# A weight ring of ten 2 MB pairs in place of nine, with areas taken from head tiles, the scatter matrix and overflow scratch

## The chip, the cores and the metric

The kernel runs on one core of a Trainium2 chip. The metric is the device time of one execution in microseconds. The profile was taken on one execution of the same program.

## The reference

All arrays are float32, with 256 tokens of width 1024. Two blocks follow each other:

```
x = x + mix(rmsnorm(x)) @ w_out            # pooling mixer beside latent attention
h = rmsnorm(x)
top4 = top_k(h @ w_router + b_router, 4)   # 32 experts, softmax over the four
x = x + sum_e gate_e * (swiglu(h @ w_gate_up[e] + b_gate_up[e]) @ w_down[e] + b_down[e])
x = rmsnorm(x)
# block 2: modulation from c @ w_ada, three kinds of attention, then a gated FFN of width 2816
```

An expert has 2048 columns of gate and up weights over 1024 rows (8 MB) and a down matrix of 1024 by 1024 (4 MB). All 32 experts are read: 384 MB of the 494 MB that the kernel moves.

## The kernel before, in words

**Stages.** `head()` computes the first mixer and the routing, `moe()` the 32 experts one after the other, `block2()` the second block. Each stage has its own pool of tiles in SBUF (`hp`, then `mp` with `ep`, then `bp`); they lie on the left side, above the constants and the ring, one in the place of the other. `ep` lies on the right side and ends at the end of the space. A tile of a later pool waits for the last readers and writers of those earlier tiles that lie on its addresses (`reuse_waits="tile"`), and for no others.

**The ring.** Weights go through slots of 1 MB (8,192 bytes per partition). Slots are numbered so that 2i and 2i+1 are the two halves of area `space[i]`; slot 12 is a single one, `space[6]` having half the size. A list, `loads`, holds all loads in the order in which the program needs them. `pump()` (line 227) gives the next load the first free slot, or the first free pair if it is larger than 1 MB, and issues its DMA on SyncE, whose program order is kept; it stops when there is none. `release()` frees slots and calls `pump()`. So every load waits, on SyncE, for the last reader of its slots, and behind it wait all later loads.

**Depth.** In the head the slots are 0 to 9 and 12; the areas 10 and 11 hold activations. `deepen()` (line 263) is called at the start of `moe()`: it adds three areas `extra0` to `extra2` in `ep` (slots 14 to 19) and slots 10 and 11, and then nine pairs are in use. An expert takes four loads of 2 MB for gate and up (`gu`, e, k) and two for down (`dn`, e, k); they are loaded as gu(e), dn(e-1). From gu(31,4) on (`LAST`), only slots 0 to 5 and 8 are given out (`KEPT`), since the others change their use in block 2.

**Addresses.** Bytes per partition, as the allocator places them in the kernel before:

| what | from | to |
|---|---|---|
| slot 12 | 104,416 | 112,608 |
| start of the left pools (`scr` in `hp`, `Pm` in `mp`) | 145,376 | |
| `hT` | 147,584 | 151,680 |
| `wh`, three buffers of 4,096 | 152,032 | 164,320 |
| `wl`, three buffers of 4,096 | 164,320 | 176,608 |
| router weights `wrt` | 176,768 | 177,792 |
| `extra0`, `extra1`, `extra2` | 180,192 | 229,344 |

The routing (line 939) takes the second and third `wl` buffer again for `eq`, one for each half of the tokens, writes their first 512 bytes and reduces them at line 957.

**The order of an expert.** In `gate_up(e)` 64 matmuls of 64 weight columns accumulate; a pair is released after each second k. At k = 1 the products of expert e-2 are scattered back, at k = 5 the activations of e-1 are transposed. `down(e-1)` follows. For each group of four experts `select` (line 1006) compares ranks with a counter into `Pm`; GpSimd copies `Pm` twice side by side into the tile `gF`, and `scat_T` (line 1059) transposes that into the scatter matrix `ST`. The bias of the down projection is loaded as one small load after gu(1,6) and added at expert 1.

**Overflow.** After expert 20 the kernel tests on all engines whether an expert has more than 64 tokens, and if so computes the rest in `overflow()` (line 1227). The inputs don't reach that.

Of the kernel before, what the change touches and what calls it, by code (L numbers as in the profile page):

```python
# [10 lines left out]
F32 = mybir.dt.float32  # L11
F32R = mybir.dt.float32r
BF = mybir.dt.bfloat16
# [7 lines left out]
P = 128  # L21
T = 256
NT = 2
# [15 lines left out]
SPL = (6, 7, 12)  # L39
BIG = (10, 11)  # L40
YAT = 9
EXTRA = (14, 15, 16, 17, 18, 19)

VECS = (("g_attn_norm", 8), ("g_q_a", 2), ("g_kv_a", 1), ("g_out_pool", 4), ("g_out_attn", 4), ("g_ffn_norm", 8),
        ("norm1_g_2", 8), ("norm2_g_2", 8), ("ml_conv_w_2", 16), ("ml_conv_b_2", 4), ("c_2", 8), ("ml_h_g_2", 2),
# [103 lines left out]
ADA = [(0, 2048, k, 1) for k in range(8)] + [(2048, 2048, k, 1) for k in range(8)] + [  # L149
    (4096, 1024, k, 2) for k in range(0, 8, 2)] + [(5120, 1024, k, 2) for k in range(0, 8, 2)]  # L150
HEAD = ('ada', 'ada', 'ada', 'pool', 'ada', 'ada', 'ada', 'ada', 'ada', 0, 1, 4, 6)
BD_AT = (1, 6)
MODE = "ddddpppp" "pppppppp" "ddpp" "pppp"
GRPS = (0, 8, 16, 20, 24)
STEPS = (3, 2, 0, 0)
# [12 lines left out]
class Net:  # L168
    def __init__(self, ctx, tc, a, out):
        self.tc, self.nc, self.a, self.out = tc, tc.nc, a, out  # L170
        self.const = ctx.enter_context(tc.tile_pool(name="const", bufs=1))
        self.ringp = ctx.enter_context(tc.tile_pool(name="ring", bufs=1))
        self.uid = 0
        self.space = [None] * 7
        self.phase(F32, 0, 1, 2, 3, 4, 6)
        self.phase(F32R, 5)
        self.slots, self.held_by = sorted(KEPT + SPL + (YAT,)), {}
        self.kept = set(KEPT)
        self.turn = {"s": 0, "b": 0, "c": 0}

        self.ps = ctx.enter_context(tc.tile_pool(name="ps", bufs=4, space=PSUM))
        self.loads, self.tiles = [], {}
        self.issued = 0
# [60 lines left out]

    def phase(self, dt, *which):
        for i in which:
            self.space[i] = self.ringp.tile([P, RING_W * (1 if i == 6 else 2)], dt, name=self.nm("ring"), tag=f"ring{i}", bufs=1)

    def next_of(self, tag, dt=F32R):
        i = self.turn[tag]  # L250
# [11 lines left out]

    def deepen(self, ep):
        self.phase(F32, 5)
        self.space += [ep.tile([P, 2 * RING_W], F32, name=f"extra{i}") for i in range(len(EXTRA) // 2)]
        self.slots += EXTRA + BIG
        self.pump()

    def chunk(self, key):
        return self.tiles[key]  # L270
# [275 lines left out]
    def head(self):  # L546
        nc, c = self.nc, self.const
        tl = self.tl
        with self.tc.tile_pool(name="hp", bufs=1, reuse_waits="tile") as hp:
            scr = tl(hp, [P, D], "scr", 1, BF)  # L550
            self.route_tiles(hp)
            Hh = self.big([P, KD, T], F32R)
# [444 lines left out]
    def moe(self):  # L997
        nc, c, tl = self.nc, self.const, self.tl
        with self.tc.tile_pool(name="mp", bufs=1, reuse_waits="tile") as mp, \
                self.tc.tile_pool(name="ep", bufs=1, side="right", reuse_waits="tile") as ep:  # L1000
            self.deepen(ep)
            xg, ST, pend = {}, {}, {}
            PM, PD = {}, {}
            acts, turned = {}, {}

            def select(g):
                e0 = g * GRP
                Pm = tl(mp, [P, NT, GRP, CAP], "Pm", 1, F32R)
                for tt in range(NT):
                    nc.vector.tensor_tensor(Pm[:, tt], self.rk[:, tt, e0:e0 + GRP][:, :, None].to_broadcast([P, GRP, CAP]),  # L1010
                                            self.iota_c[:, None, :].to_broadcast([P, GRP, CAP]), op=OP.is_equal)
                PM[g] = Pm
                PD[g] = tl(mp, [P, NT, GRP, 2, CAP], "gF", 1)
                for tt in range(NT):
                    for s in range(2):
                        nc.gpsimd.tensor_copy(PD[g][:, tt, :, s], Pm[:, tt])

            def scale(g):
                rg = tl(mp, [P, 512], "rg")[:, :GRP * CAP]
                p = self.tr()  # L1020
                for tt in range(NT):
                    self.mm(p[:, :256], self.rf[:, tt:tt + 1].to_broadcast([P, P]),
                            PM[g][:, tt].rearrange("p a b -> p (a b)").bitcast(F32), tt == 0, tt == 1)
                nc.scalar.copy(rg, p[:, :256])
                return rg
# [32 lines left out]

            def scat_T(g):
                s_ = tl(mp, [P, GRP, T], "ST", 1, F32R)  # L1060
                Pd = PD.pop(g)
                for e in range(0, GRP, 2):
                    p = self.tr()
                    for j in range(2):
                        for tt in range(NT):
                            nc.tensor.transpose(p[:, j * T + tt * P:j * T + (tt + 1) * P],
                                                Pd[:, tt, e + j].rearrange("p a b -> p (a b)"), self.ident)
                    nc.vector.tensor_copy(s_[:, e:e + 2, :], p.rearrange("p (a b) -> p a b", a=2))
                ST[g] = s_

# [32 lines left out]
            def down(e):  # L1103
                aT = turned.pop(e)
                pd = self.tr()
                n = 2 if e == E - 1 else 4
                for k in range(KD):
                    w = self.chunk(("dn", e, k - k % n))
                    for s in range(2):
                        nc.tensor.matmul(pd[64 * s:64 * s + 64, :], lhsT=aT[:, k % 4, (k // 4) * 64:(k // 4) * 64 + 64],  # L1110
                                         rhs=w[:, k % n, s * 512:(s + 1) * 512], start=k == 0, stop=k == KD - 1,
                                         skip_group_check=True)
                    if k % n == n - 1:
                        self.release(("dn", e, k + 1 - n))
                yh, yl = tl(mp, [P, 512], "ys", 1, F32R), tl(mp, [P, 512], "yl", 1, F32R)
                i = nc.scalar.copy(yh, pd)  # L1116
                j = nc.vector.tensor_tensor(yl, pd, yh, op=OP.subtract)  # L1117
                if e == E - 1:
                    keep = self.tc.keep_in_program_order
                    keep(i)  # L1120
                    keep(j)
                    self.phase(F32R, 3, 5, 6)
                    w = self.chunk(("fv", 0))
                    self.pre = [(w[:, 2 * q:2 * q + 2, :], *self.halves(w[:, 2 * q:2 * q + 2, :], self.pair("bs"[q])))
                                for q in range(2)]
                    for w, hi, lo in self.pre:
                        keep(nc.scalar.copy(hi, w))
                pend[e] = yh, yl
# [34 lines left out]
            for e in range(E):  # L1163
                hooks = {}
                if e - 2 in pend:
                    hooks[SCAT_AT] = lambda e=e: scatter(e - 2)
                if e - 1 in acts:
                    hooks[TURN_AT] = lambda e=e: turn(e - 1)
                gate_up(e, rg, hooks)
                rg = None  # L1170
                if e - 1 in turned:
                    down(e - 1)
                if e == 0:
                    self.counts(mp)
                    self.late_constants()
                if e % GRP == 1 and e // GRP not in ST:
                    scat_T(e // GRP)
                if e == 1:
                    b_down()
                if e % GRP == GRP - 2 and e // GRP + 1 < E // GRP:  # L1180
                    select(e // GRP + 1)
                    rg = scale(e // GRP + 1)
                if e in (OVF, E - 1):
                    turn(e)
                    scatter(e - 1)
                    if e // GRP not in ST:
                        scat_T(e // GRP)
                    down(e)
                if e == OVF:
                    scatter(e)  # L1190
                    self.overflow(mp)
                if e == E - 3:
                    self.gF = tl(mp, [P, D], "gF")
                    self.rowbc(self.gF, self.vcol("g_final", 0, KD))
            self.y = self.granule(YAT).rearrange("p (a b) -> p a b", a=NT)
            self.s = self.const.tile([P, NT, 4], F32, name="sz")
            scr = tl(mp, [P, D], "gc", 1, BF)

            def sums(tt, h):
                x, y, s = self.x, self.y, self.s[:, tt]  # L1200
# [23 lines left out]
        nc.vector.scalar_tensor_tensor(sg, sg, 1.0, uc, op0=OP.add, op1=OP.mult)  # L1224
        return sg

    def overflow(self, mp):
        nc, tc, a = self.nc, self.tc, self.a
        wm = a["moe"]
        bg = a["b_gate_up"].rearrange("l e n -> (l e) n")  # L1230
# [6 lines left out]
        def expert(e, tt, hT):  # L1237
            pd = [self.acc(), self.acc()]
            for n in range(2):
# [7 lines left out]
                gu = []  # L1247
                for i in range(2):
                    c = i * 1024 + n * 512
                    b = mp.tile([P, 512], F32, name=self.nm("ob"), tag=("rg", "ys")[i], bufs=1)  # L1250
                    nc.sync.dma_start(b, bg[bass.ds(e, 1), c:c + 512].to_broadcast([P, 512]))
                    nc.vector.tensor_tensor(b, ps[i], b, op=OP.add)
                    gu.append(b)
# [15 lines left out]
        m = nc.values_load(self.cmax[0:1, 0:1], min_val=0, max_val=T)  # L1269
        with tc.If(m > CAP):  # L1270
            for tt in range(NT):
                hT = self.tl(mp, [P, KD, P], "gF", 1)
                for g in range(0, KD, 4):
                    h = self.tl(mp, [P, 512], "ys", 1)
                    sl = slice(g * P, g * P + 512)
                    nc.vector.tensor_tensor(h, self.hh[:, tt, sl], self.hl[:, tt, sl], op=OP.add)
                    nc.vector.tensor_scalar(h, h, self.rf[:, tt:tt + 1], None, op0=OP.mult)
# [54 lines left out]
    def block2(self):  # L1332
        nc, x, tl = self.nc, self.x, self.tl
        with self.tc.tile_pool(name="bp", bufs=1, reuse_waits="tile") as bp:
            s, y = self.s, self.y
            v = tl(bp, [P, NT, 2], "vz")
            self.adat = iter(ADAT + (20,) * 20)
# [506 lines left out]
def build(ctx, tc, a, out):  # L1844
# [1 line left out]
    n.plan_loads()  # L1846
    n.last = [l[0] for l in n.loads].index(LAST)
    n.constants()
    n.pump()
    n.ada_setup()  # L1850
    n.head()
    n.moe()
    n.block2()
# [23 lines left out]
```

## Time and profile before

| | us |
|---|---|
| runs | 1409.63, 1412.65, 1408.57 (median 1409.63) |
| the profiled execution | 1412.59 |
| its span, first to last instruction | 1410.9 |

| engine | busy us | share of the span |
|---|---|---|
| TensorE (PE) | 1301.2 | 92% |
| VectorE (DVE) | 556.1 | 39% |
| ScalarE (ACT) | 313.1 | 22% |
| GpSimd (POOL) | 61.4 | 4% |

The DMA engines moved 494.00 MB, 349 GB/s over the span. The head ends at about 115 us, the experts at about 1045 us. A busy PE is not a PE at its peak, since matmuls are pipelined. DMA share is the mean busy share of the 16 DMA engines and can come out a little above 1.

### The profile page before, as it was taken

The page shows a single profiled execution, that of the slowest core. Times are in us where ns is not written, and L with a number is a line of the kernel's source. Part 1 is how long each engine was busy: PE and PEld are TensorE (multiplying, and loading weights), DVE is VectorE, ACT ScalarE, POOL GpSimd, SP SyncE. Part 2 cuts the span into 40 slices and gives each one's busy share as a digit, 9 for nine tenths or more (in the row PEclk, how much of TensorE's full clock was granted, in tenths as well). Part 3 has the DMA queues.
Part 4 walks back from the last instruction along what each step waited for, and adds up shares of the span by engine and source line. Part 5 has one row for each costly group of instructions (what it writes and reads, how often), then busy time and mean ns, then how long its engine had stood idle before and what let it go on. Part 6 is the DMA issues. An engine that isn't in the chain of part 4 may idle for free. (4 is left out here: it accounts for less than half of the span.)

```text
span 1410.9 us, 16725 instructions
## 1 busy us (share of the span) xinstructions
PE 1301.2 (92%) x6758; PEld 699.4 (50%) x6759; DVE 556.1 (39%) x1164; ACT 313.1 (22%) x603; POOL 61.4 (4%) x194
## 2 busy tenths in 40 slices
PE   7898999999999989889878998988889999999998
PEld 6675343333333333224222433323238887799997
DVE  6664323323222223122211322222247877655555
ACT  5561000000000000000000000000035556544443
POOL 5401000000000000000000000000000000000000
PEclk9999999999999999999999999999999999999999
DMA  9679999999999999999998999999997464545520
GB/s 346 236 288 381 428 428 425 428 425 428 425 428 426 427 427 426 427 426 428 425 425 362 427 426 427 426 427 428 421 369 311 175 249 154 209 176 192 193 98 30
DMA packets 43811, 494.00 MB, mean 350 GB/s; under 512 B 6192, under 2 KB 6320, under 8 KB 10064
## 3 DMA queue, kind: packets, MB, share of 16 engines
q1 hardware_dynamic: 41808, 492.12, 84.1%
q8 instruction: 55, 0.90, 0.3%
q10 hardware_dynamic: 1920, 0.75, 0.2%
q14 instruction: 28, 0.23, 0.0%
HBM read 491.81 MB, written 1.05 MB: 349 GB/s over the span
## 5 line engine op out<-in xcount | busy, mean ns | idle before, releaser
L1082 PE MATMUL acc<-ring,xg 128*64 128x512 f32 x1408 | 326.0, 608 | 22.9 <-DMA ring<-in_moe_dram 21.9
L1082 PEld LDWEIGHTS acc<-ring,xg 128*64 128x64 f32 x1408 | 98.0, 139 | 225.8 <-issue 181.9
L1110 PE MATMUL tr<-ring,aT 128*64 128x512 f32 x688 | 154.7, 596 | 7.4 <-DMA ring<-in_moe_dram 6.7
L301 DVE TENSOR_TENSOR ring<-ring,ring 128x1024 fp32r<-128x1024 f32 (+4 forms) x108 | 121.1, 1130 | 87.4 <-ACT ring L300 84.0
L1082 PE MATMUL acc<-extra,xg 128*64 128x512 f32 x640 | 147.4, 609 | 6.2 <-DMA extra<-in_moe_dram 6.2
L286 PEld LDWEIGHTS tr<-cols,ring 128*128 128x128 f32 x1056 | 128.1, 192 | 1.7 <-ACT cols L1327 0.8
L286 PE MATMUL tr<-cols,ring 128*128 128x256 f32 x1056 | 128.9, 283 | 0.0
L300 ACT CAST ring<-ring 128x1024 fp32r<-128x1024 f32 (+4 forms) x108 | 104.1, 974 | 103.9 <-PE tr L286 65.9
L1141 DVE SCALAR_TENSOR_TENSOR x<-tr,G,x 128x512 f32<-128x512 f32 x128 | 87.7, 744 | 76.5 <-PE tr L1137 76.5
L1220 DVE TENSOR_SCALAR gc<-acc 128x512 f32<-128x512 f32 x32 | 22.1, 691 | 239.6 <-PE acc L1082 239.6
L1117 DVE TENSOR_TENSOR yl<-tr,ys 128x512 fp32r<-128x512 f32 x32 | 22.1, 691 | 205.7 <-ACT ys L1116 205.7
L1110 PEld LDWEIGHTS tr<-ring,aT 128*64 128x64 f32 x688 | 48.3, 137 | 98.5 <-issue 85.1
L1221 ACT ACTIVATE sg<-gc 128x512 f32<-128x512 f32 x32 | 20.2, 631 | 339.6 <-DVE gc L1220 339.6
L1082 PEld LDWEIGHTS acc<-extra,xg 128*64 128x64 f32 x640 | 44.6, 140 | 96.6 <-issue 82.2
L1110 PE MATMUL tr<-extra,aT 128*64 128x512 f32 x336 | 76.1, 597 | 2.2 <-DMA extra<-in_moe_dram 1.9
L1116 ACT CAST ys<-tr 128x512 fp32r<-128x512 f32 x32 | 18.7, 585 | 240.6 <-PE tr L1110 240.6
L1099 ACT ACTIVATE aT<-tr 128x512 f32<-128x512 f32 x32 | 19.1, 597 | 232.6 <-PE tr L1097 232.6
L286 PE MATMUL acc<-ring,cols 128*128 128x384 f32 (+3 forms) x384 | 69.3, 330 | 1.2 <-ACT cols L1327 0.6
L286 PEld LDWEIGHTS acc<-ring,cols 128*128 128x128 f32 x384 | 61.3, 188 | 9.0 <-issue 5.7
L1037 DVE SCALAR_TENSOR_TENSOR xg<-tr,vt,rg 128x256 f32<-128x256 f32 x60 | 26.2, 479 | 91.3 <-PE acc L1082 74.6
L286 PE MATMUL acc<-ring,q 128*128 128x512 f32 x176 | 56.7, 394 | 0.0
L286 PE MATMUL acc<-wh,ring 128*128 128x512 f32 (+1 forms) x128 | 42.3, 410 | 4.0 <-ACT wh L307 3.8
(432 smaller groups left out, 1294.7 us busy)
## 6 DMA issues: line engine op xcount, KB each, us to landing
ring<-in_moe_dram SPq DMA_DIRECT2D x129, 2048.0 KB, 34.4
extra<-in_moe_dram SPq DMA_DIRECT2D x61, 2048.0 KB, 35.0
ring<-in_rest_dram SPq DMA_DIRECT2D x69, 1024.0 KB, 6.9
ring<-in_rest_dram SPq DMA_DIRECT2D x11, 768.0 KB, 5.7
ring<-in_moe_dram SPq DMA_DIRECT2D x4, 1024.0 KB, 12.8
ring<-in_rest_dram SPq DMA_DIRECT2D x2, 832.0 KB, 9.7
ring<-in_rest_dram SPq DMA_DIRECT2D x2, 780.0 KB, 12.1
ring<-in_rest_dram SPq DMA_DIRECT2D x3, 512.0 KB, 8.5
```

The source lines that it names most:

```text
L286: self.nc.tensor.matmul(out, lhsT=l, rhs=r, start=start, stop=stop, skip_group_check=True)
L300: i = nc.scalar.copy(hi, w)
L301: j = nc.vector.tensor_tensor(lo, w, hi, op=OP.subtract)
L1037: nc.vector.scalar_tensor_tensor(x[:, j, :], p[:, j * 256:(j + 1) * 256], self.vcol("g_ffn_norm", k + j), rg, op0=OP.mult, op1=OP.mult)
L1082: nc.tensor.matmul(d[64 * s:64 * s + 64, :], lhsT=xg[g, k - k % 2][:, k % 2, i * CAP:(i + 1) * CAP], rhs=w[:, o + s * 512:o + (s + 1) * 51 ...
L1099: nc.scalar.activation(aT.rearrange("p a b -> p (a b)"), p, AF.Copy, scale=0.5)
L1110: nc.tensor.matmul(pd[64 * s:64 * s + 64, :], lhsT=aT[:, k % 4, (k // 4) * 64:(k // 4) * 64 + 64], rhs=w[:, k % n, s * 512:(s + 1) * 512], ...
L1116: i = nc.scalar.copy(yh, pd)
L1117: j = nc.vector.tensor_tensor(yl, pd, yh, op=OP.subtract)
L1141: ins = nc.vector.scalar_tensor_tensor(d, p, self.G[:, tt, e:e + 1], d, op0=OP.mult, op1=OP.add)
L1220: nc.vector.tensor_scalar(gc, pg, 7.0, None, op0=OP.min)
L1221: nc.scalar.activation(sg, gc, AF.Tanh, scale=0.851)
```

## The change

`EXTRA` gets slots 20 and 21, a fourth area of `ep`, and ten pairs serve the experts. Slot 12 leaves the ring's own pool and is a tile of the stage's pool: the first of `hp` in the head, and of `bp` in block 2; during the experts it doesn't exist. The copy of `Pm` in `gF` falls away: `scat_T` multiplies `Pm` by the identity, once for each half of the output partitions. The tiles `ys` and `yl` fall away: the two halves of the down projection's result use `gc` and `uc` of the SwiGLU. The row of the final norm's gains takes the place of `hh`. The overflow branch takes as its scratch the pair of dn(20,4), which is released after the test, not before. The bias of the down projection is loaded after gu(9,6) and added at expert 9. The first `pump()` and `ada_setup()` are called at the start of `head()`.

```diff
-EXTRA = (14, 15, 16, 17, 18, 19)
+EXTRA = (14, 15, 16, 17, 18, 19, 20, 21)
...
-BD_AT = (1, 6)
+BD_AT = (9, 6)
...
-        self.phase(F32, 0, 1, 2, 3, 4, 6)
+        self.phase(F32, 0, 1, 2, 3, 4)
...
-            self.space[i] = self.ringp.tile([P, RING_W * (1 if i == 6 else 2)], dt, name=self.nm("ring"), tag=f"ring{i}", bufs=1)
+            self.space[i] = self.ringp.tile([P, RING_W * 2], dt, name=self.nm("ring"), tag=f"ring{i}", bufs=1)
...
     def deepen(self, ep):
         self.phase(F32, 5)
+        self.slots.remove(12)
         self.space += [ep.tile([P, 2 * RING_W], F32, name=f"extra{i}") for i in range(len(EXTRA) // 2)]
         self.slots += EXTRA + BIG
         self.pump()
+
+    def borrow(self, pool, dt):
+        self.space[6] = pool.tile([P, RING_W], dt, name=self.nm("ring"))
...
         with self.tc.tile_pool(name="hp", bufs=1, reuse_waits="tile") as hp:
+            self.borrow(hp, F32)
+            self.pump()
+            self.ada_setup()
             scr = tl(hp, [P, D], "scr", 1, BF)
...
                 PM[g] = Pm
-                PD[g] = tl(mp, [P, NT, GRP, 2, CAP], "gF", 1)
-                for tt in range(NT):
-                    for s in range(2):
-                        nc.gpsimd.tensor_copy(PD[g][:, tt, :, s], Pm[:, tt])
 
             def scale(g):
-                rg = tl(mp, [P, 512], "rg")[:, :GRP * CAP]
+                rg = tl(mp, [P, GRP * CAP], "rg")
...
             def scat_T(g):
                 s_ = tl(mp, [P, GRP, T], "ST", 1, F32R)
-                Pd = PD.pop(g)
                 for e in range(0, GRP, 2):
                     p = self.tr()
                     for j in range(2):
                         for tt in range(NT):
-                            nc.tensor.transpose(p[:, j * T + tt * P:j * T + (tt + 1) * P],
-                                                Pd[:, tt, e + j].rearrange("p a b -> p (a b)"), self.ident)
+                            for s in range(2):
+                                self.mm(p[64 * s:64 * s + 64, j * T + tt * P:j * T + (tt + 1) * P],
+                                        PM[g][:, tt, e + j].bitcast(F32), self.ident, True, True)
                     nc.vector.tensor_copy(s_[:, e:e + 2, :], p.rearrange("p (a b) -> p a b", a=2))
                 ST[g] = s_
...
-                    if k % n == n - 1:
+                    if k % n == n - 1 and (e, k) != (OVF, KD - 1):
                         self.release(("dn", e, k + 1 - n))
-                yh, yl = tl(mp, [P, 512], "ys", 1, F32R), tl(mp, [P, 512], "yl", 1, F32R)
+                yh, yl = tl(mp, [P, 512], "gc", 1, F32R), tl(mp, [P, 512], "uc", 1, F32R)
...
-                    self.phase(F32R, 3, 5, 6)
+                    self.phase(F32R, 3, 5)
...
-                if e == 1:
+                if e == BD_AT[0]:
                     b_down()
...
                 if e == OVF:
                     scatter(e)
-                    self.overflow(mp)
+                    self.overflow(mp, self.granule(self.held_by["dn", e, 4][0], 2))
+                    self.release(("dn", e, 4))
                 if e == E - 3:
-                    self.gF = tl(mp, [P, D], "gF")
+                    self.gF = self.big([P, 1, D], F32, "c")[:, 0]
                     self.rowbc(self.gF, self.vcol("g_final", 0, KD))
             self.y = self.granule(YAT).rearrange("p (a b) -> p a b", a=NT)
             self.s = self.const.tile([P, NT, 4], F32, name="sz")
-            scr = tl(mp, [P, D], "gc", 1, BF)
+            scr = tl(mp, [P, D], "sg", 1, BF)
...
-    def overflow(self, mp):
+    def overflow(self, mp, room):
...
-                    b = mp.tile([P, 512], F32, name=self.nm("ob"), tag=("rg", "ys")[i], bufs=1)
+                    b = room[:, 1024 + 512 * i:1536 + 512 * i]
...
-                hT = self.tl(mp, [P, KD, P], "gF", 1)
+                hT = room[:, :1024].rearrange("p (a b) -> p a b", a=KD)
                 for g in range(0, KD, 4):
-                    h = self.tl(mp, [P, 512], "ys", 1)
+                    h = room[:, 2048:2560]
...
         with self.tc.tile_pool(name="bp", bufs=1, reuse_waits="tile") as bp:
+            self.borrow(bp, F32R)
...
     n.constants()
-    n.pump()
-    n.ada_setup()
     n.head()
     n.moe()
     n.block2()
```

## Rows read from the trace of the kernel before

**Rows 1.** Windows: stretch, its length, busy us (instructions) by engine, PE clock, DMA share, GB/s.
```profile
core 0: us, PE busy (x) PEld busy (x) DVE busy (x) ACT busy (x) POOL busy (x), PEclk, DMA share, GB/s
...
120.00:130.00 10.00, 10.00 (x53) 5.14 (x54) 4.48 (x17) 2.19 (x4) 0.29 (x1) 0.96 0.77 266
...
140.00:480.00 340.00, 327.11 (x1512) 121.44 (x1508) 94.52 (x151) 23.48 (x40) 8.69 (x25) 0.98 1.01 427
480.00:713.00 233.00, 207.05 (x958) 76.00 (x956) 60.83 (x96) 15.15 (x26) 4.95 (x14) 0.99 1.01 427
...
757.00:1018.00 261.00, 236.84 (x1097) 87.00 (x1095) 65.60 (x103) 18.86 (x32) 3.48 (x11) 0.98 1.01 427
```

**Rows 2.** Chain that ended last, end of the expert stage: start, length, what.
```profile
963.22 40.71 DMA ring<-in_moe_dram
...
1018.55 9.92 DMA ring<-in_moe_dram
...
1028.51 3.68 PE tr L1110 x16
```

**Rows 3.** SyncE's waits over the whole span: who, for what, total, times, longest.
```profile
SPq L241 <- PE acc L1082: 311.4, 80, 19.0
SPq L241 <- DMA ring<-in_moe_dram: 252.1, 70, 14.3
SPq L241 <- PE tr L1110: 134.5, 45, 5.3
SPq L241 <- DMA extra<-in_moe_dram: 119.4, 28, 4.5
```

**Rows 4.** Issues at 713.07 and 752.96 (start, length), then their landings (last number).
```profile
713.07 0.33 SPq L241 DMA_DIRECT2D ring<-in_moe_dram  x1
...
752.96 0.34 SPq L241 DMA_DIRECT2D ring<-in_moe_dram  x1
...
ring<-in_moe_dram SPq DMA_DIRECT2D x1, 2048.0 KB, 39.2
...
ring<-in_moe_dram SPq DMA_DIRECT2D x1, 2048.0 KB, 7.8
```

**Rows 5.** Issues of gu(1,0), gu(1,2), gu(1,6), dn(0,0), dn(0,4), gu(2,0), single windows.
```profile
98.38 0.33 SPq L241 DMA_DIRECT2D ring<-in_moe_dram  x1
...
98.80 0.38 SPq L241 DMA_DIRECT2D extra<-in_moe_dram  x1
...
99.71 0.67 SPq L241 DMA_DIRECT2D extra<-in_moe_dram  x1
...
107.67 0.34 SPq L241 DMA_DIRECT2D ring<-in_moe_dram  x1
...
127.11 0.33 SPq L241 DMA_DIRECT2D ring<-in_moe_dram  x1
...
130.54 0.33 SPq L241 DMA_DIRECT2D ring<-in_moe_dram  x1
```

**Rows 6.** The same six loads, us from issue to landing (last number).
```profile
ring<-in_moe_dram SPq DMA_DIRECT2D x1, 2048.0 KB, 7.6
...
extra<-in_moe_dram SPq DMA_DIRECT2D x1, 2048.0 KB, 13.5
...
extra<-in_moe_dram SPq DMA_DIRECT2D x1, 2048.0 KB, 23.0
...
ring<-in_moe_dram SPq DMA_DIRECT2D x1, 2048.0 KB, 20.5
...
ring<-in_moe_dram SPq DMA_DIRECT2D x1, 2048.0 KB, 8.9
...
ring<-in_moe_dram SPq DMA_DIRECT2D x1, 2048.0 KB, 10.4
```

**Rows 7.** Timeline of DVE at the end of the routing: start, length, instruction.
```profile
113.80 0.29 DVE L957 TENSOR_REDUCE sel<-wl 128x32 f32<-128x128 f32 x1
```

**Rows 8.** SyncE's instructions at the overflow test: count, ns, first and last start.
```profile
L1270 SPq EVENT_SEMAPHORE  x9: 17/17/17, 719.7 to 752.5; - x9
```

**Rows 9.** Weight loads of the scatter matrix's transposes: count, ns min/median/max.
```profile
L1066 PEld LDWEIGHTS tr<-ident,gF x64: 137/141/146, 160.3 to 967.6; 128*128 128x128 f32 x64
```

**Rows 10.** Gate and up matmuls on ring tiles: busy, mean ns, idle before, releaser.
```profile
L1082 PE MATMUL acc<-ring,xg 128*64 128x512 f32 x1408 | 326.0, 608 | 22.9 <-DMA ring<-in_moe_dram 21.9
```

More of the change, by code (lines that the diff above doesn't have):

```diff
@@ L1002, in moe @@
             xg, ST, pend = {}, {}, {}
-            PM, PD = {}, {}
+            PM = {}
             acts, turned = {}, {}
```

## The prediction

> **What bounds the kernel now.** I read the windows first, then the chain of waits, then SyncE's own waits, and last the issues of single loads.
> The reader is to see four things.
> In the windows, the expert stage moves 427 GB/s at a DMA share of 1.01 from 140 us to the end of the experts, in the part where PE is busy 327 of 340 us and in the part where it is busy 207 of 233 [rows 1]. So one 2 MB load costs 2.097 MB / 427 GB/s = 4.9 us, and the stage is as long as its loads.
> The chain ends the stage on them: a load of 40.7 us, matmuls, a load of 9.9 us, then the last down projections [rows 2]. Block 2 follows on PE, so a shift of the load stream passes to the end one to one.
> SyncE waits on PE's releases in 80 + 45 cases, but in 70 + 28 on the landing of an older load [rows 3]. A load issued at 713.07 us, before the overflow test, takes 39.2 us [rows 4], which is 8 loads of 4.9 us. So 8 loads, 16 MB, are in flight at most, and in that part of the stage a ring of 18 MB is already larger than what can be under way.
> What the ring's depth costs today is then a hole in the stream, and I find one inside the expert stage before the overflow test. dn(0,0) lands at 107.67 + 20.5 = 128.2, the next load, dn(0,4), at 127.11 + 8.9 = 136.0 [rows 5, 6]: 7.8 us in place of 4.9, about 3 us lost (266 GB/s from 120 to 130 us [rows 1]), because no pair was free before gu(0,0) was used.
>
> **The start of the expert stage, where the sum is made.** The right-hand pool grows from three areas of 16,384 bytes per partition to four and ends at the same 229,344, so `extra0` moves from 180,192 down to 229,344 - 65,536 = 163,808 and reaches to 180,192. The head's tiles keep their addresses: the area that held slot 12 leaves the ring (the left pools begin 8,192 bytes lower) and comes back as the first tile of the head's pool. `extra0` now lies on all three `wl` buffers (164,320 to 176,608) and on the router weights. Two of the `wl` buffers are the routing's `eq`, whose last reader is DVE's reduction at L957, 113.80 + 0.29 = 114.1 us [rows 7]. In the kernel before, nothing that late lay under an extra area: the first extra load went out 0.4 us behind gu(1,0) [rows 5].
> The slots are handed out in the order 14, 15, ..., so the first load after `deepen`, gu(1,2), takes `extra0` and waits until 114.1 instead of going at 98.80. SyncE issues in order: behind it stand gu(1,4), gu(1,6), dn(0,0) and dn(0,4), whose areas are free (the last since 107.67 [rows 5]). The bias load is no longer among them.
> When the stream starts from rest, the first load lands 7.6 us after its issue and the second 112.3 - 106.0 = 6.3 us later [rows 5, 6]; then 4.9 each. From 114.1: 121.7, 128.0, 132.9, 137.8, and dn(0,4) at 142.7. gu(2,0) needs gu(0,0)'s pair as dn(0,4) did, free at 127.1, and follows at 147.6. Before it landed at 130.54 + 10.4 = 140.9 [rows 5, 6]. Shift: **+6.7 us**. It contains the closed hole (about -3) and the dropped bias load; the 15.3 us of blocked queue outweigh both. PE does not stall: from gu(0,0)'s release at 127.1 it frees a pair every 3.4 us at best (130.54 - 127.11 [rows 5]) and has nine more to use before gu(2,0), wanted at about 127.1 + 9 x 3.4 = 158 us.
> If the area came free before that, the queue's next wait is the one that ended at 107.67 us [rows 5], and the shift +0.3; I take the row's 114.1, as no later instruction of the head reads under the area.
> The Trainium skill, "DMA: Bandwidth & Descriptors", section on the anatomy of one DMA, gives a DMA that GpSimd issues about 2.0 us fixed plus bytes at 436 GB/s. By it five loads from 114.1 would end at 140.2 and the shift be 4.1 us (an estimate from that page); the two starts from rest in the trace take 7.6 and 7.8 us to the first landing and 6.3 to the second [rows 4 to 6], so I go by those.
>
> **The bias load moved to expert 9.** b_down's load sits between gu(1,6), landed 99.71 + 23.0 = 122.7, and dn(0,0), 128.2 [rows 5, 6]: 5.5 us for both, 0.5 above a plain load. It is left out of the chain above and comes back at expert 9: **+0.5 us**. Bounds: +0.3 (128 KB at 427 GB/s) and +4.9 (one load's place lost, as it takes half of a pair until it is used); I take the row's 0.5, since the ring has then the nine pairs of today.
>
> **The overflow test at expert 20.** SyncE waits there until every load in flight has landed: 9 waits from 719.7 to 752.5 us [rows 8]; the load issued at 713.07 lands at 752.3, and the next one 7.8 us after the restart at 752.96 [rows 4], 760.8. That hole is about 5 us: 760.8 - 752.3 - 4.9 = 3.6 at the first load and 6.3 - 4.9 = 1.4 at the second. The change holds back one release and has one pair more, so the same load, dn(21,0), is the last one out, and 8 stay in flight. Gain **0**; bounds -5 (hole gone) and +1.
>
> **Scatter matrix, scratch, end.** Per group 8 transposes become 16 matmuls with 64 weight columns. The weight load of a transposing matmul is 141 ns long [rows 9], and the matmuls overlap with it, so 16 advance at about 16 x 0.14 = 2.2 us against 8 x 0.14 = 1.1: +1.1 us in 8 places, under the loads, as PE is idle for 26 of 233 us [rows 1]. Uncovered, 9 us. The copies of POOL fall away; nothing waits for POOL long. `gc` and `uc` now also carry the down projection's halves: they are written after the SwiGLU of the next expert and read in the gate projection after that, so no order tightens. `gF` goes where `hh` stood, done since expert 27. At the end the fixed pairs come round: gu(31,4) gets (0,1) from gu(30,2), earlier than now; dn(30,4) still needs gu(31,4)'s pair, issued 5.0 us before its predecessor lands (1018.55 + 9.92 - 4.9 [rows 2]), more than the 2.7 us of a start (7.6 - 4.9). Block 2 has the same slots. **0** for all; bounds -0.5 and +9.
>
> **Sum.** +6.7 + 0.5 = +7.2 us. The profiled execution took 1412.59 us (span 1410.9, 1.7 around it): 1419.8. It lies 2.96 above the median of 1409.63, near the slowest of the three, so against the median: **1416.8 us**.
>
> **Rivals.**
> *The first extra area is free at once* (place: gu(1,2)'s issue). Then the hole at 128 closes and nothing is paid: dn(0,4) goes at 107.7, gu(1,6) lands at 122.7, dn(0,0) at 127.6, dn(0,4) 132.5, gu(2,0) 137.4, 3.5 us earlier; with the bias load -3.0, 1406.6. Against it stand the addresses; for it, that a tile which is written only in its first 512 bytes could be placed or freed otherwise. It decides at an issue by 106.9 us, where gu(2,0) (issue + 33.5) and 0.5 come out even: earlier is not slower than now. Chance 0.12.
> *Too few buffers after all.* PE idles 22.9 us before the gate and up matmuls on ring tiles, 21.9 of them for the load [rows 10]; if a pair more took these away, 1409.6 - 21.9 = 1387.7. But the share of 1.01 in the same stretch says that the loads, not their room, are short. Chance 0.02. The Trainium skill, "Perfetto Trace Analysis", optimization strategy, reads a repeated gap on an engine as a possible lack of buffers; by the windows this case disagrees.
> *The overflow hole is given back*, because the tenth pair changes what is out at the test: 1416.8 - 5 = 1411.8. Against it: 8 in flight either way. Chance 0.06.
> *PE pays for the matmuls* of the scatter matrix in the open: 1416.8 + 9 = 1425.8. Chance 0.05.
>
> **How the numbers follow.** Forecast 0.75. Three runs of before span 0.3%, so I count 0.3%, 4.2 us, as the least difference to tell. Slower: 0.75 less 0.04 for a shift under 4.2 us, plus 0.05 = 0.76. Same: 0.04, the overflow case 0.06, and 0.08 of the free area = 0.18. Faster: 0.04 of it and 0.02 = 0.06. The forecast's own range is 1413.5 to 1419.5; to leave out no more than 0.2 I reach down to 1409 into the mixed cases and up to 1420.
>
> **What would show it.** Right: the first extra load issues at about 114.1 us, released by DVE L957; no load lands between 106 and 121; from gu(2,0) on the stream lies 6.5 to 7.5 us later and stays so through the overflow test and to the last down load; no hole at 128; SyncE's waits on landings as many as now. Wrong: an extra load issued near 99 us, a stream that is earlier at 140 us, or an overflow hole that is much shorter than 5 us.

## The result, and the profile of the changed kernel

| | before | changed | ratio, 95% interval |
|---|---|---|---|
| median us, six runs each side | 1410.16 (1407.06 to 1412.65) | 1417.85 (1413.85 to 1419.91) | 1.0055 (1.0036 to 1.0075) |
| the same, a second set of runs | 1406.43 (23 runs) | 1414.71 (6 runs) | 1.0052 (1.0038 to 1.0067) |

The change costs 7.8 us (1410.16 x 0.0055; 5.1 to 10.6). The profiled execution of the changed kernel took 1413.85 us (span 1412.1), the fastest of its six, and its span is only 1.2 us longer than the one shown of before. The difference must therefore be read from the load stream, not from the two spans.

The routing's last reduction on DVE's timeline (start us, length, instruction, count):

```profile
110.97 0.29 DVE L964 TENSOR_REDUCE sel<-wl 128x32 f32<-128x128 f32 x1
```

L964 is the line that was L957 [rows 7]; it ends at 111.26. SyncE's wait just before the load that goes out next, and what ended it:

```profile
SPq L241 <- DVE sel L964: 2.2, 1, 2.2
```

SyncE's timeline from the start of expert 1:

```profile
94.76 0.33 SPq L241 DMA_DIRECT2D ring<-in_moe_dram  x1
111.36 1.94 SPq L241 DMA_DIRECT2D extra<-in_moe_dram  x4
113.34 11.13 SPq L241 DMA_DIRECT2D ring<-in_moe_dram  x2
...
124.14 0.33 SPq L241 DMA_DIRECT2D ring<-in_moe_dram  x1
```

These are gu(1,0); gu(1,2), gu(1,4), gu(1,6) and dn(0,0) together; dn(0,4) and gu(2,0) together; and gu(2,0) by itself. gu(1,2) goes out 0.10 us behind the reduction, with the loads that had stood behind it right after. Where gu(1,2) followed gu(1,0) by 0.42 us [rows 5], it now follows by 16.60. The landings of gu(1,0), gu(1,2), dn(0,4) and gu(2,0), last number us from issue:

```profile
ring<-in_moe_dram SPq DMA_DIRECT2D x1, 2048.0 KB, 7.8
...
extra<-in_moe_dram SPq DMA_DIRECT2D x1, 2048.0 KB, 7.6
...
ring<-in_moe_dram SPq DMA_DIRECT2D x1, 2048.0 KB, 26.0
...
ring<-in_moe_dram SPq DMA_DIRECT2D x1, 2048.0 KB, 20.1
```

gu(1,0) lands at 102.5, and nothing more until gu(1,2) at 118.95. dn(0,4) lands at 139.3 and gu(2,0) at 144.2, 4.9 apart: the hole at 128 us [rows 5, 6] is gone.

Windows of the changed kernel (columns as in [rows 1]):

```profile
120.00:130.00 10.00, 10.00 (x49) 3.34 (x49) 3.20 (x14) 1.82 (x3) 0.29 (x1) 1.00 1.01 431
140.00:480.00 340.00, 321.28 (x1552) 121.50 (x1550) 93.73 (x149) 23.48 (x40) 4.52 (x13) 0.99 1.01 425
480.00:713.00 233.00, 205.88 (x1024) 78.12 (x1022) 61.65 (x98) 15.16 (x26) 1.76 (x6) 1.00 1.01 427
757.00:1018.00 261.00, 235.17 (x1130) 88.73 (x1130) 69.14 (x109) 19.49 (x33) 2.05 (x7) 0.98 1.00 423
```

120 to 130 us went from 266 to 431 GB/s. The later stretches move 423 to 427, as before; in the last one the stream restarts from the overflow test at 758 us, inside the window. SyncE's waits over the span (who, for what: total us, times, longest):

```profile
SPq L241 <- DMA ring<-in_moe_dram: 384.5, 88, 10.6
SPq L241 <- DMA extra<-in_moe_dram: 244.7, 57, 5.8
SPq L241 <- PE acc L1085: 129.8, 40, 10.2
...
SPq L241 <- PE tr L1113: 58.0, 22, 5.3
```

145 waits now end on a landing, 98 did [rows 3]; 62 end on PE's releases, 125 did. With the tenth pair a slot is free earlier, and the load then waits for an older load's landing instead. In the trace SyncE's loads report their landings on eight semaphores in turn, and before each load SyncE waits for the semaphore that this load will use, that is, for the landing of the load eight places before it; in both kernels no load goes out sooner than 0.06 us after that landing. So the eight loads in flight that the prediction counted are the program's eight semaphores. Whether the hardware would take more, no run shows. The overflow test: SyncE's waits there, the last issue before it (dn(21,0)) and the first after it (dn(21,4)), and their landings:

```profile
L1274 SPq EVENT_SEMAPHORE  x9: 17/17/17, 724.6 to 757.6; - x9
...
718.13 0.33 SPq L241 DMA_DIRECT2D extra<-in_moe_dram  x1
...
758.07 0.34 SPq L241 DMA_DIRECT2D extra<-in_moe_dram  x1
...
extra<-in_moe_dram SPq DMA_DIRECT2D x1, 2048.0 KB, 39.2
...
extra<-in_moe_dram SPq DMA_DIRECT2D x1, 2048.0 KB, 8.9
```

Nine waits again, and 767.0 - 757.3 - 4.9 = 4.8 us lost at the first load (the second lands 4.7 us behind it, with no further loss), against 3.6 + 1.4 = 5.0 from [rows 4]. The end of the expert stage in the chain of waits:

```profile
988.87 29.59 DMA ring<-in_moe_dram
...
1022.20 10.98 DMA ring<-in_moe_dram
1033.22 3.68 PE tr L1113 x16
```

As in [rows 2], a load ends the stage: 4.7 us later by the clock of the span (1033.22 against 1028.51), and 8.3 us later counted from gu(1,0)'s issue, which came 3.6 us earlier in this execution.

Counting from gu(1,0)'s issue is what makes the kernels comparable. The table gives, for the profiled execution of each kernel below, three stretches of the load stream, worked out from the issues and landings of single loads as in [rows 5, 6].

| us | gu(1,0) issue to gu(2,0) landing | to gu(20,0) | to the last down load |
|---|---|---|---|
| before | 42.6 | 532.7 | 364.8 |
| changed | 49.4 | 534.6 | 364.4 |
| changed, run again | 48.6 | 534.6 | 365.8 |
| before with the wait | 51.8 | 532.6 | 364.6 |
| nine pairs | 42.2 | 535.4 | 364.7 |
| first area last | 38.4 | 534.0 | 364.3 |
| the same, run again | 38.1 | 534.1 | 364.4 |
| bias load alone | 41.3 | 534.5 | 364.8 |
| scatter matrix alone | 42.3 | 533.4 | 364.4 |
| first area last, bias at 1 | 42.2 | 532.9 | 364.5 |
| first area last, no bias | 38.3 | 532.7 | 365.8 |
| first area last, bias by ScalarE | 38.2 | 533.7 | 364.3 |

Changed against before: +6.9, +1.9, -0.5, together +8.3 us; run again, +6.1, +1.9, +0.9, together +8.9 us. What lies outside the stream, gu(1,0)'s issue at 94.5 to 98.4 us and 369.0 to 372.5 us behind the last load, varies by up to 4 us between executions, in kernels with and without the change, and in the profile of before both are at the long end (98.4 and 372.5). That is why the two spans stand only 1.2 us apart.

### The profile page after: what moved, and what is told of

Read it like the earlier page. It is cut to its first block, busy times and chain, and to the rows that moved or that the text cites. A ratio compares the mean times of both kernels' runs of the same rounds, so it can differ in the third digit from the quotient of the medians.

```text
span 1412.1 us, 17071 instructions
## 1 busy us (share of the span) xinstructions
PE 1297.1 (92%) x6950; PEld 703.7 (50%) x6951; DVE 556.4 (39%) x1164; ACT 313.2 (22%) x603; POOL 49.6 (4%) x162
## 5 line engine op out<-in xcount | busy, mean ns | idle before, releaser
L1085 PE MATMUL acc<-ring,xg 128*64 128x512 f32 x1296 | 296.6, 605 | 17.4 <-DMA ring<-in_moe_dram 17.2
L1085 PEld LDWEIGHTS acc<-ring,xg 128*64 128x64 f32 x1296 | 89.1, 139 | 199.5 <-issue 161.7
L1085 PE MATMUL acc<-extra,xg 128*64 128x512 f32 x752 | 172.6, 605 | 14.4 <-DMA extra<-in_moe_dram 14.4
L1113 PE MATMUL tr<-ring,aT 128*64 128x512 f32 x608 | 137.4, 597 | 9.4 <-DMA ring<-in_moe_dram 9.0
L1085 PEld LDWEIGHTS acc<-extra,xg 128*64 128x64 f32 x752 | 51.8, 139 | 120.8 <-issue 94.2
L1120 DVE TENSOR_TENSOR uc<-tr,gc 128x512 fp32r<-128x512 f32 x32 | 22.1, 692 | 210.3 <-ACT gc L1119 210.3
L1113 PE MATMUL tr<-extra,aT 128*64 128x512 f32 x416 | 93.8, 596 | 2.9 <-DMA extra<-in_moe_dram 2.6
L1113 PEld LDWEIGHTS tr<-ring,aT 128*64 128x64 f32 x608 | 43.0, 137 | 87.1 <-issue 71.5
L1119 ACT CAST gc<-tr 128x512 fp32r<-128x512 f32 x32 | 18.7, 585 | 245.9 <-PE tr L1113 245.9
L1113 PEld LDWEIGHTS tr<-extra,aT 128*64 128x64 f32 x416 | 29.7, 137 | 57.0 <-issue 51.7
## 6 DMA issues: line engine op xcount, KB each, us to landing
ring<-in_moe_dram SPq DMA_DIRECT2D x117, 2048.0 KB, 39.2
extra<-in_moe_dram SPq DMA_DIRECT2D x73, 2048.0 KB, 39.2
```

What stands on the lines that cost most here:

```text
L1085: nc.tensor.matmul(d[64 * s:64 * s + 64, :], lhsT=xg[g, k - k % 2][:, k % 2, i * CAP:(i + 1) * CAP], rhs=w[:, o + s * 512:o + (s + 1) * 51 ...
```

## The experiments

My theory: the first extra area makes the head of SyncE's queue wait for the routing, and that is nearly the whole loss. The rivals: the other edits (bias load, scatter matrix, scratch) cost it, or ten pairs as such do.

**The changed kernel again** (label after_again) beside the first experiments, as a mark.

> The changed kernel, unedited, timed on the same chip as the three kernels beside it. My theory (the first load into extra0 waits for the end of the routing and holds up SyncE's queue, 6.7 us, and the bias load costs 0.5 at its new place): 7 us above the kernel before. Rivals (the edits of scatter matrix, scratch and bias cost it, or the deeper ring itself does): the same here, so this run only gives the mark for the others.

1414.71 us, ratio 1.0052 (1.0038 to 1.0067): +7.3 us. The loss is there again.

**The first area handed out last** (label extra0_last).

```diff
-        self.slots += EXTRA + BIG
+        self.slots += EXTRA[2:] + BIG + EXTRA[:2]
```

> The changed kernel with its free slots handed out in the order 16 to 21, 10, 11, 14, 15, so that extra0 is the last area filled. My theory: gu(1,2) issues about 0.4 us behind gu(1,0); extra0 goes to dn(0,4), whose turn comes near the routing's end; no hole between gu(1,0) and gu(2,0). gu(2,0) lands about 4 us earlier than in the kernel before, measured from gu(1,0), and with 0.5 us for the bias load the time is 3.5 us under the kernel before, 10.5 under the changed one. If the other edits cost the time: 7 us above before, as the changed kernel. If the ring's depth itself costs: 7 us above too.

1405.27 us, ratio 0.9992 (0.998 to 1.0005): 9.4 us under the changed kernel. SyncE's timeline there:

```profile
95.23 0.33 SPq L241 DMA_DIRECT2D ring<-in_moe_dram  x1
95.65 1.56 SPq L241 DMA_DIRECT2D extra<-in_moe_dram  x3
104.53 0.33 SPq L241 DMA_DIRECT2D ring<-in_moe_dram  x1
111.11 0.33 SPq L241 DMA_DIRECT2D extra<-in_moe_dram  x1
123.59 10.63 SPq L241 DMA_DIRECT2D ring<-in_moe_dram  x4
```

The area is still not free before 111 us, but now dn(0,4) takes it. Of the five loads issued ahead of it three have not landed yet (gu(1,4), gu(1,6) and dn(0,0)), so the stream doesn't stop. One line of order turns the loss into nothing or a small gain. The stream reaches gu(2,0) 4.2 us earlier than before, as expected; of the 3.5 us expected in the time, 1.2 were measured, and the interval (2.8 us under to 0.7 over) leaves out 3.5. A second set of runs, below, does not.

**The wait put into the kernel before** (label before_wait): a write to the first extra area (`space[7]`) by DVE, behind the routing's reduction.

```diff
         self.space += [...]
+        self.nc.vector.tensor_copy(self.space[7][:, 0:1], self.sel[:, 1, 0:1])
         self.slots += EXTRA + BIG
```

> The kernel before with one small DVE copy from the routing's sel into extra0 ahead of the first extra load, so that this load must wait for the routing's end as in the changed kernel; nine pairs, all else as before. My theory: gu(1,2) issues about 0.3 us after the last reduction of the routing, about 15.5 us later than in the kernel before, and from gu(2,0) on the loads land 7.4 us later: 7.4 us above before. If the other edits of the change cost the time: within 1 us of before.

1415.31 us, ratio 1.0057 (1.0042 to 1.0072): +8.0 us. Issues of the first extra load and of gu(2,0), and their landings:

```profile
111.67 0.33 SPq L241 DMA_DIRECT2D extra<-in_moe_dram  x1
...
126.00 0.33 SPq L241 DMA_DIRECT2D ring<-in_moe_dram  x1
...
extra<-in_moe_dram SPq DMA_DIRECT2D x1, 2048.0 KB, 7.7
...
ring<-in_moe_dram SPq DMA_DIRECT2D x1, 2048.0 KB, 20.3
```

gu(2,0) lands 51.8 us behind gu(1,0)'s issue, 9.2 later than in the kernel before, where I expected 7.4, and 2.4 later than in the changed kernel: about 0.6 because the wait lasts longer (gu(1,2) follows gu(1,0) by 17.2 us, not 16.6), and 1.6 from gu(1,4)'s landing to dn(0,0)'s, where the bias load still stands. The wait alone makes a loss of the change's size in a kernel with none of its other edits.

**The changed kernel with nine pairs** (label nine_pairs): every edit but the tenth pair, so that `extra0` lies where it lay.

```diff
-EXTRA = (14, 15, 16, 17, 18, 19, 20, 21)
+EXTRA = (14, 15, 16, 17, 18, 19)
```

> The changed kernel without slots 20 and 21: nine pairs, extra0 back at its old address, all other edits of the change kept. My theory: gu(1,2) issues 0.4 us behind gu(1,0) again, dn(0,4) again waits for gu(0,0)'s release, and the time is within 1 us of before. If the other edits cost it: 7 us above before. If PE paid for the scatter matrix's matmuls: up to 9 us above.

1408.79 us, ratio 1.0015 (1.0005 to 1.0025): +2.1 us, more than I had allowed. The first area is free at once, and the hole is back:

```profile
120.00:130.00 10.00, 10.00 (x51) 3.83 (x51) 3.88 (x16) 1.82 (x3) 0.29 (x1) 1.00 0.60 224
```

At gu(2,0) it is level with before (42.2 against 42.6 us); it loses 2.8 us between there and gu(20,0). So something among the other edits costs about 2 us. Three kernels were to say which.

The kernel with the first area handed out last differs from this one by the tenth pair and its order alone. It is 3.5 us faster (1405.27 against 1408.79, 11 runs each, in one set), and its first stretch is 3.8 us shorter: that is the closed hole, and the worth of the tenth pair where nothing waits behind it.

**The bias load alone** (label bd_only), in the kernel before.

```diff
-BD_AT = (1, 6)
+BD_AT = (9, 6)
...
-                if e == 1:
+                if e == BD_AT[0]:
```

> The kernel before with one edit, the bias load and its matmuls at expert 9 instead of expert 1. Open from the runs so far: the kernel with nine pairs was 2.1 us slower than before although its stream reached expert 2 no later, and it lost this between experts 2 and 20, most plainly from gu(8,0) to gu(10,0) (61.0 us against 60.2). Theory 'bias load' (it takes half of a pair and a place in SyncE's queue at expert 9): 1.0 to 2.0 us slower than before, and the landings of gu(8,0) and gu(10,0) 61.0 us or more apart. Theory 'scatter matrix' (16 matmuls for 8 transposes on PE): as before within 0.5 us, 60.2 us there. Theory 'scratch' (the held release and the areas of the pools): as before too, within 0.5 us.

1406.02 us against 1407.92, ratio 0.9992 (0.9981 to 1.0004): no loss. The stretch to gu(20,0) grew by 1.8 us as the theory wanted (gu(8,0) to gu(10,0) 60.5 us, less than the 61.0 expected). The time doesn't show it: 1.1 us under before (2.7 under to 0.6 over). In this trace the first stretch is 1.3 us shorter, so that the whole stream is only 0.4 us longer, but that 1.3 can't be put down to the load's old place. With nine pairs dn(0,4) and gu(2,0) wait there for PE's releases, behind the hole. Two more such kernels have nearly the same first stretch, one with the load at expert 9 (nine pairs, 42.2) and one with it at expert 1 (scatter matrix alone, 42.3).

**The scatter matrix alone** (label scat_only), in the kernel before: `select` without GpSimd's copies, and in `scat_T`

```diff
-                            nc.tensor.transpose(p[:, ...], Pd[:, tt, e + j].rearrange("p a b -> p (a b)"), self.ident)
+                            for s in range(2):
+                                self.mm(p[64 * s:64 * s + 64, ...], PM[g][:, tt, e + j].bitcast(F32), self.ident, True, True)
```

> The kernel before with one edit, the scatter matrix from 64 matmuls per group of four experts... that is, 16 matmuls in place of 8 transposes for each pair step, and without GpSimd's copies. Theory 'bias load': as before within 0.5 us, since PE waits for loads and the matmuls lie under them. Theory 'scatter matrix': 1.0 to 2.0 us slower than before, lost in steps near the experts where the matrix is built (1, 9, 17, 25). Theory 'scratch': as before within 0.5 us. What my prediction said of it: 0, and 9 us slower if nothing covers the matmuls.

1408.31 us, ratio 1.0005 (0.9993 to 1.0017): no difference that can be told, +0.7 us in the middle stretch and none over the whole stream (940.05 against 940.07 us).

**First area last, bias load back at expert 1** (label last_bias1).

```diff
-BD_AT = (9, 6)
+BD_AT = (1, 6)
```

> The changed kernel with the first extra area handed out last, and the bias load back at expert 1. It is to be compared with the kernel that has the first of these alone (1.2 us under before). Theory 'bias load': the 1 to 2 us lost near expert 9 come back, less the 0.5 us that the load takes at expert 1: 0.5 to 1.5 us under that kernel, some 2.5 us under before. Theories 'scatter matrix' and 'scratch': no gain over that kernel, 0.5 to 1.5 us under before. Either way the stream reaches gu(2,0) 3.5 to 4 us earlier than in the kernel before.

1407.65 us, ratio 0.9997 (0.9986 to 1.0009). The middle stretch is back at 532.9 us, as the theory of the bias load said, but no time was won, since gu(2,0) came at 42.2 us where I expected 38.5. SyncE's timeline shows why:

```profile
96.50 1.67 SPq L241 DMA_DIRECT2D extra<-in_moe_dram  x3
105.37 0.34 SPq L241 DMA_DIRECT2D ring<-in_b_down_dram  x1
111.94 0.34 SPq L241 DMA_DIRECT2D extra<-in_moe_dram  x1
124.77 7.19 SPq L241 DMA_DIRECT2D ring<-in_moe_dram  x3
```

The bias load takes half of the ring pair that dn(0,0) had at 104.53 in the kernel without it. dn(0,0) gets the tenth pair, and dn(0,4) waits until 124.77 for gu(0,0)'s: the hole at 128 us stays open in spite of ten pairs. It took both edits to close it.

**No bias load, and the bias by another queue** (labels last_nobias, last_bias_act; extra0_last_2 is the kernel with the first area last, run again beside them). All three are the changed kernel with the first area last.

> The kernel with the first extra area handed out last, without the bias load and without the four matmuls and four additions that use it: the down projection's bias is left out of the output. What is open: in the five kernels with the bias load at expert 9 the stream takes 534.0 to 535.4 us from gu(2,0) to gu(20,0), in the four with it at expert 1 532.6 to 533.4. Theory 'the load costs the stream 1.2 to 1.7 us where it stands' (the big load ahead of it lands about 1 us late as well): that stretch 532.6 to 533.0, and the whole 1.2 to 1.7 us under the kernel with the load. Rival 'its place is worth 0.5 us', as in my prediction: 533.5, and 0.5 us under it. Rival 'the half pair it holds costs the stream, not the load': as the first theory here, and apart only in the kernel with the load on ScalarE's queue.

> The kernel with the first extra area handed out last, and the bias taken out of the ring: two loads of 64 KB, issued by ScalarE at experts 9 and 13 into the idle place of the comparison matrix, used at experts 10 and 14. SyncE's queue and the ring hold weights alone. Theory 'the bytes and packets of the load cost the stream': as with the load in the ring, 534 us from gu(2,0) to gu(20,0), 1.2 us under before. Rival 'the place in SyncE's queue or the half pair costs it': 532.6 to 533.0, and 2.4 to 2.9 us under before, as without the load.

The second in short:

```diff
-                add(("bd",), "b_down")
+                bias[n] = tl(mp, [E, 512], "Pm")
+                nc.scalar.dma_start(bias[n], b_down[:, n * 512:(n + 1) * 512])
...
+                if e in (9, 13):
+                    b_load(e // 13)
+                if e in (10, 14):
+                    b_down(e // 13)
```

> The kernel with the first extra area handed out last once more, beside the two above, so that the three stand on one chip: 1.2 us under before, as it was, within 1 us; 534 us from gu(2,0) to gu(20,0).

| | median us | ratio to before (1408.18, 29 runs) |
|---|---|---|
| first area last, again | 1405.03 | 0.998 (0.9968 to 0.9992) |
| without the bias load | 1403.72 | 0.9976 (0.9962 to 0.9989) |
| bias by ScalarE's queue | 1405.13 | 0.9974 (0.9962 to 0.9987) |

The middle stretch falls to 532.7 us without the load (534.0 and 534.1 with it in the ring), so the load, with the matmuls that use it, makes the 1.3 to 1.4 us there. The whole stream doesn't show a gain in these traces: 936.8 us without the load, 936.7 and 936.6 with it, as the last stretch is 1.4 us longer in the trace without. By ScalarE's queue the middle stretch is 533.7, between the theories and settling neither. The three times can't be told apart. They are 0.20 to 0.26% under before: the ring of ten pairs with a mended order is a little faster than the kernel before, 3.7 us (1.8 to 5.4) in the last form. The first form is 2.8 us under before here (1.1 to 4.5), more than the 1.2 within 1 us that I expected; in the earlier set of runs it was level with before.

## Why the prediction was right

**The step that made the sum held.** An area moved under the routing's tiles, the first load in the queue took it, and the loads behind waited too. gu(1,2)'s issue was named with its releaser and came 0.10 us after it. The shift at gu(2,0) was forecast at 6.7 us and is 6.9 in the changed kernel; both counter-tests agree (the wait alone costs 8.0 us, the order alone gives 9.4 back). That the two numbers lie so close is partly luck, since two misses of opposite sign nearly cancel: gu(1,2) follows gu(1,0) by 16.6 us where the prediction has 15.7 (114.1 - 98.38), and from gu(1,2)'s issue to gu(2,0)'s landing it takes 32.8 us where it has 33.5. In the second trace of the changed kernel the shift is 6.1. In the chain itself, after the start from rest the second landing came at once 4.9 us behind the first, where I had taken 6.3, and gu(1,6) came 0.7 us late; from the first issue to dn(0,4)'s landing it is 139.3 - 111.4 = 27.9 us, I had 28.6.
The Trainium skill, "DMA: Bandwidth & Descriptors", section on the anatomy of one DMA, has a fit for DMAs that GpSimd issues, and would make that 26.1 us (2.0 + 5 x 2.097 MB at 436 GB/s, an estimate from that page). The trace has 27.9; the shift worked out with that fit, 4.1 us, lies under the 6.9 measured.

**The bias term was too small.** I took +0.5 us for the load at expert 9. Counted from rows of the load stream, it is two and a half to three times that. Issues of gu(9,4), gu(9,6), the bias load and dn(8,0) in the changed kernel, and their landings:

```profile
324.49 0.33 SPq L241 DMA_DIRECT2D ring<-in_moe_dram  x1
...
327.92 0.33 SPq L241 DMA_DIRECT2D extra<-in_moe_dram  x1
...
331.28 0.34 SPq L241 DMA_DIRECT2D extra<-in_b_down_dram  x1
...
337.10 0.34 SPq L241 DMA_DIRECT2D extra<-in_moe_dram  x1
...
ring<-in_moe_dram SPq DMA_DIRECT2D x1, 2048.0 KB, 37.0
...
extra<-in_moe_dram SPq DMA_DIRECT2D x1, 2048.0 KB, 39.7
...
extra<-in_b_down_dram SPq DMA_DIRECT2D x1, 128.0 KB, 36.8
...
extra<-in_moe_dram SPq DMA_DIRECT2D x1, 2048.0 KB, 35.7
```

They land at 361.5, 367.6, 368.1 and 372.8. Two plain loads take 9.8 us from the first to the last; here it is 11.3, 1.5 more, of which 1.2 lie in the big load ahead of the small one. In all six traces with the load at expert 9 these loads take 11.0 to 11.3 us, 1.2 to 1.5 more. I had looked only from the big load's landing on (5.5 us, 0.5 over a plain one) and so missed the lateness in front, which is in the trace of before as well: there gu(1,6) lands 5.5 us behind gu(1,4). (In the changed kernel gu(1,6) is late too, with no small load behind it, so not all of that need be the bias load's.) The stream is therefore 8.8 us later at gu(20,0) and 8.3 at its end, where I had 7.2, and leaves the 6.5 to 7.5 us that I gave as a sign. The times say 7.8 and 7.3 with 2 to 3 us on either side, and can't tell the two sums apart; no run shows the bias load's price in the time.

**The other terms.** The overflow hole stayed: 4.8 against 5.0 us, eight loads of 4.9 us in flight before the test (39.2). The matmuls of the scatter matrix were hidden: in the trace a group of them takes about 2.4 us where the transposes took 1.1, near what was reckoned (2.2 against 1.1), and nothing shows over the whole stream. Nothing was given back at the end: 364.4 us from gu(20,0) to the last down load, 364.8 before.

**The rivals.** *The first area free at once* was priced 3.0 us under before; the kernel with the order mended comes nearest to that case (the area is not free at once, but nothing waits behind it), measured at 1.2 and 2.8 us under, with its place (gu(2,0) 3.5 us earlier, measured 4.2) about right. *Too few buffers* falls: ten pairs with no early wait gain 1.2 to 3.7 us, not 21.9. *The overflow hole given back* and *PE pays* did not come.

**Wrong in the list of signs:** I expected as many waits of SyncE on landings as before, and there are 145 against 98. A ring larger than what may be in flight moves SyncE's wait from the slot to the landing of the load eight places before; the number of waits then says nothing of time. The first extra load also went out at 111.36 us, not 114.1: the head was earlier by the clock of the span in this execution, and the releaser was the one named.

**Open.** The nine-pair kernel lost 2.8 us in its middle stretch, of which the bias load explains about 1.5. The rest lies in other late landings, 0.6 to 0.9 us each, which no edit was shown to cause. The edits of the scratch (the held release, the shared tiles) were never run by themselves.

## What to carry to other kernels

When a buffer grows, look at which earlier tiles lie under its new address and when their last reader ends; then look at which load takes it first. In an in-order queue a late area at the head holds up areas that are free, and handing it out last is worth more than the buffer itself (9.4 us against 1.2 to 3.7). Where the program lets eight loads be in flight, a tenth pair bought nothing in the steady state; its use was a single hole, and a small load that breaks a pair kept that hole open. Compare two kernels by a stretch between two events of the stream and not by two spans, when a stage without any edit varies by as much as the change is worth.

## What the runs showed of the hardware

A load of 128 KB on 32 partitions cost a saturated stream of 2 MB loads 1.2 to 1.5 us at the place where it lands, where its bytes at 427 GB/s are 0.3; most of it appears as a late landing of the large load issued ahead of it. In every kernel some landings come 0.9 to 1.6 us late with no edit near them (gu(31,0) at 1003.9 us before, gu(30,6) at 993.9 in the changed kernel). In the kernel before, gu(9,4) and gu(17,4) are late, and again gu(23,0) and gu(31,0): 48 loads apart both times. What makes these was not found.
